# Sixteen of the 22 inner blocks of a feed-forward layer read a normed operand instead of the raw one

## The chip, the cores and the metric

One NeuronCore of a Trainium2 chip runs the whole program as one launch. The metric is the device time in microseconds (us), taken as the median of the runs. All operands are float32; products are made exact by splitting each operand into a high part and a low part with a shorter mantissa (hi, lo) and taking three matmuls, hi·hi, lo·hi and hi·lo.

## The reference, cut to what matters

The program computes two blocks in a row on 256 tokens of 1024 features. The change lies in the feed-forward part of the second block, which has two layers:

```python
for l in range(2):
    ...
    x = layer_norm(ALPHA * x + g1 * (o @ w_out[l]), ln1_g[l], ln1_b[l])
    x = layer_norm(ALPHA * x + g2 * swiglu(modulate(x, sh2, sc2), w_ffn_in[l], w_ffn_out[l]), ln2_g[l], ln2_b[l])

def modulate(x, shift, scale):
    return x * (1 + scale) + shift

def swiglu(u, w_ffn_in, w_ffn_out):
    a, b = jnp.split(u @ w_ffn_in, 2, axis=-1)
    return (jax.nn.silu(a) * b) @ w_ffn_out
```

`w_ffn_in` has 2 x 2816 columns, that is 22 blocks of 128 columns for `a` and 22 for `b`.

## The kernel before, in words

The tokens are kept transposed: the tile `xT` (in code `x`, `ax` or `z`) is [128 features, 8 feature blocks, 256 tokens]. At the end of the output projection a layer norm stands between `xT` and the feed-forward layer. The kernel does not wait for it. `late` (L1201) makes an operand `lh`, `ll` (hi and lo) of the tokens before their norm, with 258 columns: 256 tokens and two columns A and B of the modulation. The products of the inner layer are taken from this operand while the norm's sums, scale and offset are still being worked out. `lfin` (L1214) then finishes a product: with the norm's scale and offset (tile `ro`, one row for all partitions) it makes `t = ps * scale + offset * c` from the PSUM bank `ps` and the product's own two extra columns `c` (tiles `lt` and `lc`).

`ffn` (L1758) runs over 22 inner blocks j. For each it loads 1 MB of weights (tile `w`), splits them in two halves in `wload` (L271: `wh` by ScalarE, `wl` by VectorE; four buffers each), takes 48 matmuls into two PSUM banks (8 feature blocks x 2 x 3), and calls `fin(j)`, which has two `lfin` on VectorE, a Silu on ScalarE into tile `hj` (two buffers), a last VectorE instruction that multiplies into `hj`, and `evac` (L256), which splits the result: `hidh` on ScalarE and `hidl` on GpSimd (POOL). After most blocks one step of `modcol` (tiles `wd`, `macc`: a VectorE instruction over 1024 columns that prepares a later modulation) is put behind the last VectorE instruction of `fin`. `fin(j)` also takes one step of `apply` (L1314): for one feature block of `xT` two POOL instructions multiply by the scale and add the offset, and a third one multiplies by `ag` and adds `ab`. These 24 POOL instructions bring `xT` itself through the norm, eight steps in eight blocks.

Four loops over the 22 hidden blocks (the outer layer, from `hidh`, `hidl`) and the next norm follow.

The order on every engine is set when the program is built, by a scheduler in the recording layer that sees all the engines' queues; it may put an instruction ahead of others that the code wrote earlier. On the chip each engine goes through its own list in that order. The helpers have one line each: L236 is every matmul, L309 every ScalarE activation, L319, L322, L314 and L316 are the VectorE and POOL instructions with two inputs, three inputs, and one input with one or two scalars, and L396 the weight loads.

Of the kernel before, what the change touches and what calls it, by code (L numbers as in the profile page):

```python
# [21 lines left out]
# rows of 128 that become per-partition columns on the chip  # L22
# [15 lines left out]
# column order of the second block's input projection: 10 chunks of 256 columns  # L38
def _r(*p):
    return sum([list(range(a, b)) for a, b in p], [])  # L40
# [3 lines left out]
    _r((1152, 1408)),                                                       # linear attention: q | k  # L44
    _r((1408, 1664)),                                                       # its v
    _r((1952, 2016), (2144, 2208), (2336, 2464)),                           # grouped q, heads 0 3 | k
    _r((2016, 2080), (2208, 2272), (2080, 2144), (2272, 2336)),             # grouped q, heads 1 4 | 2 5
    _r((384, 640)),                                                         # neighbourhood k
    _r((0, 256)),                                                           # q
    _r((640, 768), (256, 384)),                                             # k | q  # L50
    _r((768, 1024)),                                                        # v
    _r((1024, 1152), (2464, 2592)),                                         # v | grouped v
    _r((1664, 1920)),                                                       # gate of the linear attention
]
# rows of the second block's output projection: query heads j and 3 + j share a tile
_WOR = list(range(640)) + sum(
    [list(range(640 + 64 * j, 704 + 64 * j)) + list(range(832 + 64 * j, 896 + 64 * j)) for j in range(3)], [])
# column order of the first block's input projection: 14 chunks of 256 columns
# [3 lines left out]
# rows of the gates on the chip: forget | input, forward heads at 0, backward heads at 32  # L62
# [3 lines left out]
def _consts():  # L66
# [4 lines left out]
    # persistent constants  # L71
# [28 lines left out]
    # masks of the levels of the linear attention  # L100
# [7 lines left out]
    # constants of the first block  # L108
# [6 lines left out]
    # frequencies at the middles of a grid of 512; tokens about their middle, folded  # L115
# [11 lines left out]
    z = np.concatenate([tl[:, None], np.cos(bw), -np.sin(bw)], -1).astype(f)   # 256, 33  # L127
# [8 lines left out]
def _layout(i):  # L136
    """numpy only moves data here"""
# [56 lines left out]
    # relative position bias as [token, key], one constant outside the window  # L194
# [8 lines left out]
    o["bias"] = pad[:, :, idx].reshape(2, 6, 2, 128, 256).transpose(0, 3, 1, 2, 4)   # l p h tt s  # L203
# [4 lines left out]
class _W:  # L208
    """a weight tile in parts of four slices"""
# [9 lines left out]
class _B:  # L219
    """one launch: both blocks"""  # L220
# [17 lines left out]
    def mx(self, out, L, R, sl, sr, start=True, stop=True):  # L238
        """one product of operands that are whole (x,) or split exactly (hi, lo)"""
        if len(L) == 1:  # L240
            self.mm(out, sl(L[0]), sr(R[0]), start, stop)
            return
        (lh, ll), (rh, rl) = [sl(x) for x in L], [sr(x) for x in R]
        self.mm(out, lh, rh, start, False)
        self.mm(out, ll, rh, False, False)
        self.mm(out, lh, rl, False, stop)

    def split(self, pool, x, tag, bufs, eng=None):
        """x = hi + lo, each with float32r's mantissa"""
# [6 lines left out]
    def evac(self, st, dst, i, x, eng=None):  # L256
        """x into slice i of an operand"""
# [6 lines left out]
    def op8(self, st, tag):  # L264
        """an operand tile [128, 8, 256]"""
# [20 lines left out]
    def bank(self, ps, w, u, q, order=range(8), half=None):  # L286
        """two blocks of 128 columns into one bank, over half of the eight row tiles: q is 0 or 4"""
# [9 lines left out]
    def pin(self, after):  # L297
        """issue what follows after these instructions, each on its own engine"""
# [41 lines left out]
    # per-token statistics of a transposed tile: sums over the feature axis as columns  # L340
# [5 lines left out]
    def rows(self, ps, colv):  # L346
        """columns [tok, 2] -> the same row on every partition [128, 256]"""
# [10 lines left out]
    def toT(self, psp, dst, src):  # L358
        """[tok, 2, 1024] -> [128, 8, 256]"""
# [13 lines left out]
    def fromT(self, psp, dst, src):  # L373
        """[128, 8, 256] -> [tok, 2, 1024]"""
# [24 lines left out]
    def modvec(self, psp, wd, lhs, bias, outs, groups, get=None):  # L399
        """lhs [128, 8, 32] against wd (1024, 6144), 1024 columns a group; outs: list of (column tile, replica)"""  # L400
# [9 lines left out]
    def modout(self, pool, psp, ps, bias, outs, g):  # L410
        """a group's products, 256 columns on each quarter of the partitions, as columns"""
# [14 lines left out]
    def modcol(self, pool, psp, wd, v, bias, out, groups):  # L426
        """column tile v [128, 8] against wd (1024, 6144), 1024 columns a group: products summed over the row tiles on
        the vector engine, then over the partitions on the tensor engine"""
# [17 lines left out]
    def run(self):  # L446
        nc, tc, d = self.nc, self.tc, self.d
        self.wbufs = {"w": 4, "wm": 4, "wx": 2, "wb": 3, "wd": 2, "split": 4}
        with ExitStack() as es:
# [5 lines left out]
            with tc.tile_pool(name="ps", bufs=1, space=PSUM) as self.pp, \  # L455
# [11 lines left out]
                with tc.tile_pool(name="M", bufs=1) as mp, tc.tile_pool(name="WB", bufs=1) as self.wb:  # L467
                    self.moe_route(mp, pm)
                    with tc.tile_pool(name="X", bufs=1, side="right") as xp:
                        # the context's part of the second block runs between the experts' loads  # L470
# [57 lines left out]
    def phase_a(self, ap, pm, pa):  # L528
        nc, d, cp = self.nc, self.d, self.cp
        T, P = self.T, self.P  # L530
# [13 lines left out]
        # the first two groups of the modulation: buffers that nothing else needs yet  # L544
# [20 lines left out]
        o = 0  # L565
# [66 lines left out]
        def half(w, b):  # L632
            """half of the rows of a weight tile, split"""
# [1329 lines left out]
```

## Time and profile before

| | us |
|---|---|
| median of 3 runs | 2240.02 (2239.44 to 2242.13) |
| span of the profiled execution | 2234.8 |
| so around the span, against the median | 5.2 |
| first feed-forward layer, first matmul to last | about 1644.6 to 1850 |
| second feed-forward layer, first matmul to last | about 2020.8 to 2226 |
| TensorE busy in the span | 1976.9 (88%) |
| VectorE busy | 967.5 (43%) |
| ScalarE busy | 630.5 (28%) |
| POOL busy | 294.9 (13%) |

The profile is of one execution; its own time outside the profiler is not listed apart from the three runs, so the span and the 5.2 us around it stand for it. Times in the rows are microseconds from the start of the span. "PEclk" is the granted share of TensorE's full clock. The two feed-forward layers lie 376.2 us apart and run through the same sequence.

### The profile page before, as it was taken

The page shows a single profiled execution, that of the slowest core. Times are in us where ns is not written, and L with a number is a line of the kernel's source. Part 1 is how long each engine was busy: PE and PEld are TensorE (multiplying, and loading weights), DVE is VectorE, ACT ScalarE, POOL GpSimd, SP SyncE. Part 2 cuts the span into 40 slices and gives each one's busy share as a digit, 9 for nine tenths or more (in the row PEclk, how much of TensorE's full clock was granted, in tenths as well). Part 3 has the DMA queues.
Part 4 walks back from the last instruction along what each step waited for, and adds up shares of the span by engine and source line. Part 5 has one row for each costly group of instructions (what it writes and reads, how often), then busy time and mean ns, then how long its engine had stood idle before and what let it go on. Part 6 is the DMA issues. An engine that isn't in the chain of part 4 may idle for free.

```text
span 2234.8 us, 33003 instructions
## 1 busy us (share of the span) xinstructions
PE 1976.9 (88%) x13588; PEld 1373.1 (61%) x13588; DVE 967.5 (43%) x1919; ACT 630.5 (28%) x1091; POOL 294.9 (13%) x334
## 2 busy tenths in 40 slices
PE   7999879987888989988898977679999998998998
PEld 2777744542345545545455531167789998778998
DVE  3665422124402101110012111159679888868974
ACT  3434321012401000000001100055545446554543
POOL 0012000001000000000000000044044216206311
PEclk9999979998988999999999987689999999999999
DMA  9677789998897999999998999963246674214652
GB/s 347 245 294 285 260 315 411 414 417 303 332 411 306 414 414 416 417 414 414 414 417 339 404 414 418 417 223 111 92 148 226 230 240 156 99 67 170 227 198 86
DMA packets 133479, 666.31 MB, mean 298 GB/s; under 512 B 14608, under 2 KB 18128, under 8 KB 86800
## 3 DMA queue, kind: packets, MB, share of 16 engines
q1 hardware_dynamic: 132192, 660.38, 76.1%
q0 software_dynamic: 1136, 3.82, 0.5%
q8 instruction: 107, 1.75, 0.3%
q14 instruction: 44, 0.36, 0.0%
HBM read 663.10 MB, written 1.05 MB: 297 GB/s over the span
## 4 chain that ended last, share of the span: by engine, by line
PE 54%; DMA 27%; DVE 9%; ACT 3%; POOL 3%; issue 3%; SPq 0%; POOLq 0%; ACTq 0%; DVEq 0%
PE ps L236 52%; DMA wm<-in_w_f 8%; DMA w<-in_w_up 5%; DMA wb<-in_w_up 4%; PE ps L306 2%; DMA w<-in_w_down 2%; DMA wb<-in_w_down 2%; POOL xT L319 2%; DVE wl L319 1%; DMA wm<-in_w_in 1%; DMA wb<-in_w_gate 1%; DMA w<-in_w_gate 1%; DVE ll L322 1%; DMA wm<-in_w_ada 1%; DMA wd<-in_w_ada 1%
## 5 line engine op out<-in xcount | busy, mean ns | idle before, releaser
L236 PE MATMUL ps<-u,wm 128*128 128x256 f32 (+1 forms) x1168 | 279.5, 400 | 8.9 <-DMA wm<-in_w_f 5.4
L236 PEld LDWEIGHTS ps<-u,wm 128*128 128x128 f32 (+1 forms) x1168 | 228.0, 198 | 78.3 <-DMA wm<-in_w_f 17.3
L319 DVE TENSOR_TENSOR wl<-w,wh 128x1024 fp32r<-128x1024 f32 (+1 forms) x194 | 239.8, 1244 | 54.8 <-ACT wh L309 54.4
L236 PE MATMUL ps<-lh,wh 128*128 128x258 f32 x848 | 244.7, 289 | 7.6 <-DVE lt L319 7.6
L236 PE MATMUL ps<-ll,wh 128*128 128x258 f32 x848 | 244.3, 288 | 5.1 <-DVE ll L322 5.1
L236 PE MATMUL ps<-lh,wl 128*128 128x258 f32 x848 | 243.8, 288 | 5.6 <-DVE wl L319 4.1
L309 ACT ACTIVATE wh<-w 128x1024 fp32r<-128x1024 f32 (+1 forms) x196 | 200.1, 1029 | 164.4 <-PE ps L236 155.1
L236 PE MATMUL ps<-w,xsel 128*32 128x512 f32 x1176 | 182.7, 666 | 38.2 <-DMA w<-in_w_up 25.1
L319 DVE TENSOR_TENSOR hid<-hid,ps 128x256 f32<-128x256 f32 (+1 forms) x38 | 20.2, 533 | 392.4 <-ACT hid L309 241.2
L236 PEld LDWEIGHTS ps<-lh,wh 128*128 128x128 f32 x848 | 164.1, 194 | 9.9 <-ACT wh L309 8.0
L236 PEld LDWEIGHTS ps<-lh,wl 128*128 128x128 f32 x848 | 164.4, 194 | 6.7 <-DVE wl L319 5.2
L236 PEld LDWEIGHTS ps<-ll,wh 128*128 128x128 f32 x848 | 164.7, 194 | 6.2 <-DVE ll L322 6.1
L236 PE MATMUL ps<-wb,xsel 128*32 128x512 f32 x872 | 136.8, 657 | 35.1 <-DMA wb<-in_w_up 22.1
L309 ACT ACTIVATE hid<-ps 128x256 f32<-128x256 f32 (+1 forms) x38 | 18.0, 473 | 402.1 <-PE ps L236 395.8
L236 PEld LDWEIGHTS ps<-w,xsel 128*32 128x32 f32 x1176 | 31.9, 113 | 136.3 <-DMA w<-in_w_up 62.2
L1112 POOL COPY px<-Pg 128x256 f32<-128x256 f32 x16 | 6.4, 397 | 803.7 <-PE ps L306 783.7
L322 DVE SCALAR_TENSOR_TENSOR xT<-ps,mod,xT 128x256 f32<-128x256 f32 x168 | 72.9, 478 | 77.6 <-PE ps L236 77.6
L236 PE MATMUL ps<-w,hidT 128*32 128x512 f32 x584 | 82.0, 650 | 26.7 <-DMA w<-in_w_down 21.7
L236 PE MATMUL ps<-hidh,wl 128*128 128x256 f32 x352 | 98.6, 280 | 1.6 <-DVE wl L319 1.6
L236 PE MATMUL ps<-hidh,wh 128*128 128x256 f32 x352 | 98.8, 281 | 0.0
L236 PE MATMUL ps<-hidl,wh 128*128 128x256 f32 x352 | 98.2, 279 | 0.0
L236 PEld LDWEIGHTS ps<-wb,xsel 128*32 128x32 f32 x872 | 23.5, 112 | 103.5 <-DMA wb<-in_w_up 50.3
(474 smaller groups left out, 3696.1 us busy)
## 6 DMA issues: line engine op xcount, KB each, us to landing
w<-in_w_gate SPq DMA_DIRECT2D x74, 1024.0 KB, 16.0
w<-in_w_up SPq DMA_DIRECT2D x73, 1024.0 KB, 15.4
w<-in_w_down SPq DMA_DIRECT2D x73, 1024.0 KB, 16.2
w<-in_w_f SPq DMA_DIRECT2D x60, 1024.0 KB, 4.9
wb<-in_w_up SPq DMA_DIRECT2D x55, 1024.0 KB, 15.4
wb<-in_w_down SPq DMA_DIRECT2D x55, 1024.0 KB, 15.8
wb<-in_w_gate SPq DMA_DIRECT2D x54, 1024.0 KB, 15.5
wm<-in_w_ada SPq DMA_DIRECT2D x76, 512.0 KB, 6.3
```

The costliest lines, as they stand in the source:

```text
L236: self.lm = self.nc.tensor.matmul(out, lhsT, rhs, start=start, stop=stop)
L306: self.nc.tensor.transpose(out, in_, self.ident[:k, :k])
L309: self.nc.scalar.activation(out, in_, func, **kw)
L319: return (eng or self.nc.vector).tensor_tensor(out, a, b, op)
L322: return (eng or self.nc.vector).scalar_tensor_tensor(out, in0, s, in1, op0, op1)
L1112: nc.gpsimd.tensor_copy(px.rearrange("p t (r s) -> p t r s", r=4), self.Pg[:, :, e, :].unsqueeze(2).to_broadcast([128, 2, 4, 32]))
```

## The change

`ffn` makes a second operand `un` (tiles `AT` for hi and `ul` for lo, 256 columns). `apply` is now called with it: beside its three POOL instructions, each of its eight steps has a ScalarE instruction that writes the hi part of a block of `un` from the normed `xT`, a VectorE instruction (tile `Pm`) that forms the same value in full, and a second one that subtracts to give the lo part `ul`. Each `fin` takes two steps of `apply` instead of one, and what is left is taken before block 6. Blocks 0 to 5 still use the raw operand, blocks 6 to 21 use `un`, with 256 columns, and need no `lfin`: Silu is read from one PSUM bank and one VectorE instruction multiplies by the other.

```diff
     def norm(self, p, psp, z, sqtag, put=None):
...
-        sq = self.T(p, [128, 8, 256], sqtag)
+        sq = None
...
         def feed(k=None):
+            nonlocal sq
             g = nc.gpsimd
+            if sq is None:
+                sq = self.T(p, [128, 8, 256], sqtag)
...
     def ffn(self, st, l, u, ax, g, feed=None):
         p, psp, d = st["p"], st["g"], self.d
+        nl = 6
+        if st["r3"]:
+            un = (self.T(st["ap"], [128, 8, 256], st["atag"], 1, F32R), self.T(p, [128, 8, 256], "ul", 1, F32R))
...
         def fin(j, pp):
             h = self.T(p, [128, 256], "hj", 2)
-            t, c = self.lfin(p, pp[0], ro)
-            self.act(h, t, AF.Silu, bias=c)
-            t, c = self.lfin(p, pp[1], ro)
-            e = self.stt(h, t, c, h, ALU.add, ALU.mult)
+            if j < nl:
+                t, c = self.lfin(p, pp[0], ro)
+                self.act(h, t, AF.Silu, bias=c)
+                t, c = self.lfin(p, pp[1], ro)
+                e = self.stt(h, t, c, h, ALU.add, ALU.mult)
+            else:
+                self.act(h, pp[0][:, 0:256], AF.Silu)
+                e = self.tt(h, h, pp[1][:, 0:256], ALU.mult)
             self.evac(st, hid, j, h, self.nc.gpsimd)
...
-            next(app, None)
+            for _ in range(2):
+                next(app, None)
         for j in range(22):
...
                 pp = [self.P(psp), self.P(st["S"])]
+                if j == nl:
+                    self.all(app)
+                v, n = (u, 258) if j < nl else (un, 256)
...
-                            self.mx(pp[b][:, 0:258], w, u, lambda x: x[:, k, 128 * b:128 * b + 128], lambda x: x[:, k],
+                            self.mx(pp[b][:, 0:n], w, v, lambda x: x[:, k, 128 * b:128 * b + 128], lambda x: x[:, k],
                                     k == 0, k == 7)
...
-                            app = self.apply(p, ax, ro, st["cf"])
+                            app = self.apply(p, ax, ro, st["cf"], un)
...
+            self.pk = "DDDDDDDD"
             with self.tc.tile_pool(name=f"CF{l}", bufs=1, reuse_waits="tile") as fp:
...
-                sm = dict(st, p=fp, extra=extra, cf=cf, ro=ro)
+                sm = dict(st, p=fp, po=fp, extra=extra, cf=cf, ro=ro)
```

Beside this the tile `Pm` of `apply` has 256 columns instead of 512, and comments are gone. The change moves instructions on every engine at the start of the feed-forward layer. Three places are shown, all of the first layer; the second has the same order.

On POOL, from the end of the norm on. `xT<-xT,ro` is the norm of a block of the tokens (two instructions a block), `xT<-xT,cfg,cfb` the third instruction of an `apply` step, `hidl` the low part of a finished hidden block. Before:

```order
L319 TENSOR_TENSOR xT_11_85<-xT_11_85,ro_1999_10345 128x256 x4
L316 TENSOR_SCALAR xT_11_85<-xT_11_85,cfg1616_1617_8387,cfb1617_1618_8388 128x256 x2
L319 TENSOR_TENSOR xT_11_85<-xT_11_85,ro_1999_10345 128x256 x4
L316 TENSOR_SCALAR xT_11_85<-xT_11_85,cfg1616_1617_8387,cfb1617_1618_8388 128x256 x2
L319 TENSOR_TENSOR xT_11_85<-xT_11_85,ro_1999_10345 128x256 x4
L316 TENSOR_SCALAR xT_11_85<-xT_11_85,cfg1616_1617_8387,cfb1617_1618_8388 128x256 x2
L319 TENSOR_TENSOR xT_11_85<-xT_11_85,ro_1999_10345 128x256 x3
L319 TENSOR_TENSOR hidl_1979_10243<-hj_2000_10347,hidh_1978_10242 128x256
```

And with the change:

```order
L319 TENSOR_TENSOR xT_11_85<-xT_11_85,ro_2000_10346 128x256 x10
L316 TENSOR_SCALAR xT_11_85<-xT_11_85,cfg1616_1617_8387,cfb1617_1618_8388 128x256
L319 TENSOR_TENSOR xT_11_85<-xT_11_85,ro_2000_10346 128x256 x6
L316 TENSOR_SCALAR xT_11_85<-xT_11_85,cfg1616_1617_8387,cfb1617_1618_8388 128x256 x2
L319 TENSOR_TENSOR hidl_1980_10244<-hj_2001_10348,hidh_1979_10243 128x256
```

The first `hidl` stood behind 15 instructions of two inputs and 6 of one; it now stands behind 16 and 3.

On VectorE, around the last instruction of `fin` of block 2 (`hj_2019` before, `hj_2024` with the change). `wl_2027`, `wl_2029` before and `wl_2034`, `wl_2036` with the change are the two halves of the low weights of block 3; `wl_2039`, `wl_2041` and `wl_2048`, `wl_2050` are those of block 4. Before, all four stand ahead of `hj_2019`, whose last rows are:

```order
L319 TENSOR_TENSOR wl_2029_10511<-w_2025_10504,wh_2028_10510 128x1024
L322 SCALAR_TENSOR_TENSOR hj_2005_10401<-lt_2009_10410,lc_2008_10408,hj_2005_10401 128x256
L314 TENSOR_SCALAR macc_2010_10416<-wd_2011_10417,lhs2_36_140 128x1024
L1218 COPY lc_2020_10484<-ps2017_10433 128x2
L319 TENSOR_TENSOR lt_2021_10486<-ps2017_10433,ro_1999_10345 128x256
L319 TENSOR_TENSOR wl_2039_10585<-w_2037_10582,wh_2038_10584 128x1024
L322 SCALAR_TENSOR_TENSOR lt_2021_10486<-ro_1999_10345,lc_2020_10484,lt_2021_10486 128x256
L1218 COPY lc_2022_10490<-ps2018_10434 128x2
L319 TENSOR_TENSOR lt_2023_10492<-ps2018_10434,ro_1999_10345 128x256
L319 TENSOR_TENSOR wl_2041_10589<-w_2037_10582,wh_2040_10588 128x1024
L322 SCALAR_TENSOR_TENSOR lt_2023_10492<-ro_1999_10345,lc_2022_10490,lt_2023_10492 128x256
L322 SCALAR_TENSOR_TENSOR hj_2019_10483<-lt_2023_10492,lc_2022_10490,hj_2019_10483 128x256
```

With the change:

```order
L316 TENSOR_SCALAR Pm_2031_10533<-xT_11_85,cfA1614_1615_8385,cfB1615_1616_8386 128x256
L322 SCALAR_TENSOR_TENSOR hj_2024_10506<-lt_2028_10515,lc_2027_10513,hj_2024_10506 128x256
L322 SCALAR_TENSOR_TENSOR macc_2013_10428<-wd_2029_10521,lhs2_36_140,macc_2013_10428 128x1024
L319 TENSOR_TENSOR ul_1978_10242<-Pm_2031_10533,AT_1977_10241 128x256
L319 TENSOR_TENSOR wl_2034_10541<-w_2032_10538,wh_2033_10540 128x1024
L319 TENSOR_TENSOR wl_2036_10545<-w_2032_10538,wh_2035_10544 128x1024
L316 TENSOR_SCALAR Pm_2044_10615<-xT_11_85,cfA1614_1615_8385,cfB1615_1616_8386 128x256
L316 TENSOR_SCALAR Pm_2045_10622<-xT_11_85,cfA1614_1615_8385,cfB1615_1616_8386 128x256
L319 TENSOR_TENSOR ul_1978_10242<-Pm_2044_10615,AT_1977_10241 128x256
L319 TENSOR_TENSOR ul_1978_10242<-Pm_2045_10622,AT_1977_10241 128x256
L319 TENSOR_TENSOR wl_2048_10630<-w_2046_10627,wh_2047_10629 128x1024
L319 TENSOR_TENSOR wl_2050_10634<-w_2046_10627,wh_2049_10633 128x1024
```

The four low halves of blocks 3 and 4 have gone from ahead of the last instruction of `fin(2)` to behind it; ahead of it stand six `Pm` and five `ul` of the new operand.

On TensorE, at the start of block 3 (`ps2037` and `ps2038` are its PSUM banks, `ps2051` and `ps2052` those of block 4), with the change:

```order
L236 MATMUL ps2023_10457<-ll_1941_9920,wh_2020_10452 128x258
L236 MATMUL ps2037_10548<-lh_1940_9919,wh_2033_10540 128x258
L236 MATMUL ps2038_10549<-lh_1940_9919,wh_2033_10540 128x258
L236 MATMUL ps2051_10637<-lh_1940_9919,wh_2047_10629 128x258
L236 MATMUL ps2052_10638<-lh_1940_9919,wh_2047_10629 128x258
L236 MATMUL ps2037_10548<-lh_1940_9919,wl_2034_10541 128x258
```

The second matmul of block 3 needs `wl_2034`, and all later ones of the program stand behind it; four first matmuls (two of block 3, two of block 4) stand ahead of it. Before, the matmuls of block 3 stood one behind the other.

## Rows read from the trace of the kernel before

**Rows 1.** The page, part 1: busy time of the engines in the span.

```profile
PE 1976.9 (88%) x13588; PEld 1373.1 (61%) x13588; DVE 967.5 (43%) x1919; ACT 630.5 (28%) x1091; POOL 294.9 (13%) x334
```

**Rows 2.** Busy time in stretches: PE, PEld, DVE, ACT, POOL (instructions), PEclk, DMA share, GB/s.

```profile
1764.00:1778.00 14.00, 14.00 (x119) 14.00 (x118) 12.69 (x23) 7.02 (x10) 3.35 (x3) 1.00 0.62 200
1658.58:1678.26 19.68, 19.68 (x166) 19.64 (x164) 15.24 (x23) 6.92 (x9) 19.68 (x22) 1.00 0.43 159
```

**Rows 3.** Timeline of TensorE at its stall, first layer, then second layer.

```profile
1678.16 0.28 PE L236 MATMUL ps<-ll,wh 128*128 128x258 f32 x1
1682.24 0.55 PE L236 MATMUL ps<-lh,wh 128*128 128x258 f32 x1 [3.81 <-DVE lt L319]
1683.79 0.58 PE L236 MATMUL ps<-lh,wl 128*128 128x258 f32 x1 [0.99 <-DVE wl L319]
...
2054.35 0.28 PE L236 MATMUL ps<-ll,wh 128*128 128x258 f32 x1
2058.42 0.36 PE L236 MATMUL ps<-lh,wh 128*128 128x258 f32 x1 [3.79 <-DVE lt L319]
2059.96 0.58 PE L236 MATMUL ps<-lh,wl 128*128 128x258 f32 x1 [1.19 <-DVE wl L319]
```

**Rows 4.** Who waited for whom, 1658 to 1690: total us, times, longest.

```profile
ACT hj L309 <- POOL hidl L319: 9.8, 1, 9.8
DVE hj L322 <- ACT hj L309: 5.7, 1, 5.7
PEld ps L236 <- ACT wh L309: 4.0, 1, 4.0
```

**Rows 5.** Timeline of POOL, end of the norm to the first hidden block.

```profile
1658.58 4.25 POOL L319 TENSOR_TENSOR xT<-xT,ro 128x256 f32<-128x256 f32 x4 [2.52 <-ACT ro L309]
...
1676.17 2.12 POOL L319 TENSOR_TENSOR xT<-xT,ro 128x256 f32<-128x256 f32 x3
1678.26 0.72 POOL L319 TENSOR_TENSOR hidl<-hj,hidh 128x256 fp32r<-128x256 f32 x1
```

**Rows 6.** Groups of POOL instructions, 1658.5 to 1678.3: count, busy us, mean ns.

```profile
L319 POOL TENSOR_TENSOR xT<-xT,ro 128x256 f32<-128x256 f32 x15 | 14.7, 1010 | 2.5 <-ACT ro L309 2.5
L316 POOL TENSOR_SCALAR xT<-xT,cfg,cfb 128x256 f32<-128x256 f32 x6 | 5.1, 858 | 0.0
```

**Rows 7.** Timeline of POOL, start of the second layer's mixers.

```profile
1860.10 8.49 POOL L319 TENSOR_TENSOR xT<-xT,ro 128x256 f32<-128x256 f32 x9 [3.49 <-ACT ro L309]
```

**Rows 8.** Timeline of DVE: first layer's stall, then mixers of the second layer.

```profile
1679.55 0.94 DVE L322 SCALAR_TENSOR_TENSOR hj<-lt,lc,hj 128x256 f32<-128x256 f32 x1 [5.73 <-ACT hj L309]
1680.41 1.28 DVE L322 SCALAR_TENSOR_TENSOR macc<-wd,lhs,macc 128x1024 f32<-128x1024 f32 x1
...
1684.92 1.21 DVE L319 TENSOR_TENSOR wl<-w,wh 128x1024 fp32r<-128x1024 f32 x1
...
1885.62 0.73 DVE L316 TENSOR_SCALAR Pm<-xT,cfA,cfB 128x256 f32<-128x256 f32 x2
```

**Rows 9.** TensorE, timeline: 68 matmuls of 258 columns, then 70 of 256, first and last.

```profile
1759.83 0.28 PE L236 MATMUL ps<-lh,wl 128*128 128x258 f32 x1
...
1767.89 0.28 PE L236 MATMUL ps<-ll,wh 128*128 128x258 f32 x1
...
1807.76 0.28 PE L236 MATMUL ps<-hidh,wl 128*128 128x256 f32 x1
...
1815.89 0.28 PE L236 MATMUL ps<-hidh,wl 128*128 128x256 f32 x1
```

**Rows 10.** Granted clock after the stall, first and second layer: PE, PEclk, DMA share, GB/s.

```profile
1680.90:1687.80 6.90, 4.57 (x20) 0.51 0.35 93
...
2059.80:2063.20 3.40, 3.23 (x15) 0.50 0.29 113
```

**Rows 11.** VectorE groups, 1450 to 2235: count, busy us, mean ns of one.

```profile
L322 DVE SCALAR_TENSOR_TENSOR lt<-ro,lc,lt 128x256 f32<-128x256 f32 x88 | 46.3, 530 | 2.1
L319 DVE TENSOR_TENSOR lt<-ps,ro 128x256 f32<-128x256 f32 x88 | 36.2, 415 | 4.6 <-ACT ro L309 4.6
```

More of the change, by code (lines that the diff above doesn't have):

```diff
@@ L1321, in apply @@
             if u and self.pk[k] == "A":
-                y = self.T(p, [128, 512], "Pm", 3)[:, 0:256]
+                y = self.T(p, [128, 256], "Pm", 3)
                 self.stt(y, z[:, k], A[:, k:k + 1], r, ALU.mult, ALU.mult)
@@ L1333, in apply @@
             if u and self.pk[k] != "A":
-                y = self.T(p, [128, 2, 256], "hsq", 1)[:, 0] if self.pk[k] == "P" else self.T(p, [128, 512], "Pm", 3)[:, 0:256]
+                y = self.T(p, [128, 2, 256], "hsq", 1)[:, 0] if self.pk[k] == "P" else self.T(p, [128, 256], "Pm", 3)
                 self.act(u[0][:, k], z[:, k], AF.Identity, scale=A[:, k:k + 1], bias=B[:, k:k + 1])
```

## The prediction

> **What bounds the kernel now.** I read the page's first part, then busy time by stretches, then TensorE's timeline where the second view shows it not full, then the waits and the other engines' timelines around that place. TensorE is busy for 88% of the span [rows 1]. Inside the feed-forward layers it is full nearly throughout: in a stretch of steady blocks it is busy 14.00 of 14.00 us while VectorE is busy 12.69 and POOL 3.35 [rows 2]. There, only fewer or shorter matmuls can save time.
>
> The exception is the start of each layer. TensorE starts a matmul at 1678.16, the next at 1682.24 and the one after it, which needs a low weight half, at 1683.79 [rows 3]; the second layer repeats this 376.2 us later. These are the first matmuls of block 5, since blocks 3 and 4 ran before the hole. The cause is a chain of single waits [rows 4]: ScalarE waited 9.8 us for POOL to take `hidl` of block 0 out of `hj` (two buffers, so block 2 needs that of block 0), VectorE then waited 5.7 us for ScalarE's `hj`, and TensorE waited 4.0 us for weights that stood behind `hj` on ScalarE. POOL itself was full from 1658.58 to 1678.26, 19.68 of 19.68 us [rows 2], with 15 two-input instructions in 14.7 us and 6 one-input ones in 5.1 us [rows 6]. So POOL's queue ahead of the first `hidl` sets the hole; what VectorE and TensorE have queued behind block 2's `fin` sets its price.
>
> **The change, part by part.**
>
> Columns: in 16 blocks of each layer a matmul has 256 columns instead of 258. That is 16 x 48 = 768 matmuls a layer. From first to last, 67 steps of 258 columns take 8.06 us, 120.3 ns each, and 69 steps of 256 columns 8.13 us, 117.8 ns each [rows 9]. The gain is 768 x 2.5 ns = 1.9 us a layer, all of it on the path, since TensorE is full there. The Trainium skill ("TensorE: Matmul & The Clock Gate", "Back-to-back issue gap") gives an isolated matmul N / 2.4 ns and a constant. Two columns would be an estimated 0.8 ns by it, or 0.6 us a layer; the trace's spacing differs, and it decides.
>
> VectorE's relief: the same blocks lose two `lfin` each. Per block that is two instructions of 0.415 us and two of 0.530 us [rows 11], about 30 us a layer. I cost it at nothing: TensorE is already full beside that work [rows 2]. What is late next there is TensorE itself.
>
> The new operand: 8 ScalarE and 16 VectorE instructions a layer. A `Pm` costs 0.37 us in the rows for the mixers [rows 8]; the subtraction is of the kind at 0.415 us [rows 11]. By themselves they are 6 us of VectorE. What matters is where they stand: they need normed blocks, which POOL delivers one at a time, and the order has put six `Pm` and five `ul` ahead of the last instruction of `fin(2)`, and both low halves of blocks 3 and 4 behind it. TensorE's list holds four first matmuls that need high halves alone, and then one that needs block 3's `wl`. So TensorE now stops after block 2 and four matmuls, and must wait for a chain that in the old order had 96 matmuls beside it.
>
> When that chain ends: the norm is on chip at 1658.58, where POOL starts [rows 5]. Now 16 two-input and 3 one-input instructions stand ahead of `hidl`. At the rates of the old stretch, 14.7 / 15 = 0.98 and 5.1 / 6 = 0.85 us [rows 6], they take 15.7 + 2.6 = 18.3 us, to 1676.9. Nine two-input instructions in 8.49 us in the mixers [rows 7] say 0.94, the same within 0.6 us in all. `hidl` takes 0.72 [rows 5]: 1677.6. In the old run, from the end of `hidl` (1678.26 + 0.72 = 1678.98) over `hj` on ScalarE and VectorE to the end of `macc` (1680.41 + 1.28 = 1681.69) took 2.7 us [rows 5, 8]; the same instructions follow now. Then one `ul` (0.4) and the low half (1.21 [rows 8]) add 1.6. The low half is there at 1677.6 + 2.7 + 1.6 = **1681.9**.
>
> Against the old run, which took its own second matmul of block 5 at 1683.79, TensorE restarts 1.9 us earlier but two blocks behind. It has 96 matmuls more to do, less the three that now run early, 93 x 0.1203 = 11.2 us. Nothing else can run in the hole, since TensorE's list is in order. After the old hole the granted clock is 0.51 for 6.9 us in the first layer and 0.50 for 3.4 us in the second, the lower of its two levels (1.2 of 2.4 GHz) [rows 10], after 4 us without matmuls. The new hole is some 15 us long; I take the same loss after it, so no difference, and as a bound one more slow stretch of 3.4 us, which costs half of itself, 1.7 us. POOL's and ScalarE's other moves, the DMAs of weights (now queued behind two `macc` loads on SP) and the rest of the order have slack behind the restart: the four buffers of split weights let the engines run two blocks, 11 us, ahead. The last block of `un` is ready a few us after the restart, and block 6 comes 136 matmuls later.
>
> Sum a layer: -1.9 + 11.2 - 1.9 = +7.4 us; two layers +14.8. The sum is a difference in the profiled execution, whose span is 2234.8; the median, 5.2 us above it, I move by the same amount: 2240.0 + 14.8 = **2254.8**.
>
> Bounds of the unknown, POOL's pace beside VectorE. Undisturbed, three two-input instructions took 2.12 us, 0.71 each [rows 5]. All 19 at that pace take 13.5 us; the low half is ready at 1677.1, and a layer loses 2.6 us. The other end adds up the work of both engines: beside the 13.5 us, VectorE has 6 `Pm` (2.2), 5 `ul` (2.1), 6 `lt` and 2 `hj` at 0.53 (4.2) and a `macc` (1.28), 9.8 us in all. That puts the low half at 1686.9 and the loss at 12.4. I take the pace of the old stretch because VectorE was busy 15.24 of 19.68 us there [rows 2], and its instructions now in the same stretch add up to about as much.
>
> **The rivals.**
>
> *POOL and VectorE exclude each other.* If no VectorE instruction with two inputs in SBUF can run beside a POOL instruction, the upper end above holds: 2 x 12.4 = +24.8, 2264.8. For it: POOL's pace is 0.71 beside an idle VectorE and 4.25 / 4 = 1.06 beside a busy one [rows 5]. Against it: the old stretch held 19.8 us of POOL's work and 15.24 us of VectorE's in 19.68 us [rows 2, 6]; 21 instructions at 0.71 leave under 5 us for VectorE if nothing overlapped. The Trainium skill ("SBUF — State Buffer", "Who interferes with whom") states just such a lock for the whole instruction. The trace agrees that there is contention, not that it is full. Chance 0.14.
>
> *POOL runs undisturbed.* VectorE now waits for POOL's blocks, so it could leave POOL alone more than before. Lower end: 2 x 2.6 = +5.2, 2245.2. For it: VectorE's `Pm` wait for blocks one after another. Against it: the work it has in between. Chance 0.12; about half of it would show as no change.
>
> *Faster: TensorE's restart costs nothing.* If the low half were ready before the hole costs more than the old one, only the columns count: 2 x 1.9 = -3.8, and 2236.2. The point from which it decides is 1683.8 - 11.2 = 1672.6 for the low half in the first layer. That needs POOL's first `hidl` done by 1668.3, 19 instructions and `hidl` in 9.7 us, 0.49 us each; the least the rows show is 0.71. Only a VectorE that took `wl_2034` without standing behind `hj_2024` could do it, and the order excludes that. Chance 0.05.
>
> **How the numbers follow.** The forecast case, low half between 1680 and 1684 (2251 to 2259 with both layers), has 0.69, the others as given. About 0.2%, 4.5 us, is what a measurement of this kernel can tell from no change: the three runs spread over 2.7 us. The forecast and the exclusion case are slower, and so is half of the undisturbed one: 0.69 + 0.14 + 0.06 = 0.89. The same: 0.06. Faster: the last rival, 0.05, though its gain is near the limit. The range goes from the undisturbed case less the spread of the runs, 2243, to the exclusion case with a slow stretch more in each layer, 2268.
>
> **What would show it.** In the changed kernel's profile TensorE should have a hole in each layer that begins near 1667 (96 matmuls of 0.12 us before 1678.2) and ends near 1682 (and 376 + 7 us later), broken only by four single matmuls; the matmul after it should wait for VectorE's `wl`; ScalarE's wait for `hidl` should remain, several us long; POOL should be full from 1658.6 to about 1677. The matmuls from `AT`/`ul` should stand 117 to 118 ns apart. VectorE should be well under 12 of 14 us busy in the later blocks with nothing gained by it. I am wrong if the hole ends before 1677 or after 1687, if a second hole follows at blocks 5 to 7 (weights or `un` late), or if the later blocks' spacing falls by clearly more than 2.5 ns.

## The result, and the profile after

The changed kernel takes 2251.22 us (median, 2246.95 to 2256.14); the kernel before, beside it, 2239.44 us. The ratio of the runs is 1.0063, with a 95% interval of 1.0049 to 1.0078, so +14.1 us; the quotient of the two medians is 1.0053, or +11.8 us, and lies in that interval. The forecast was 2254.8 us, +14.8, and slower. The span of the profiled execution is 2244.8 us, 10.0 more than before.

The page's first part, after. VectorE has lost 31.5 us of busy time against [rows 1]; the span grew all the same:

```profile
PE 1972.9 (88%) x13588; PEld 1366.1 (61%) x13588; DVE 936.0 (42%) x1759; ACT 637.4 (28%) x1107; POOL 285.4 (13%) x334
```

Busy time in two stretches (PE, PEld, DVE, ACT, POOL with their instructions, PEclk, DMA share, GB/s), after. The first answers to the second row of [rows 2], from the start of POOL's work to the end of the first `hidl`; the second is a stretch of steady blocks:

```profile
1657.03:1673.33 16.30, 9.56 (x74) 8.82 (x72) 15.10 (x28) 10.27 (x16) 16.30 (x21) 0.84 0.09 29
1764.00:1778.00 14.00, 14.00 (x122) 14.00 (x121) 9.24 (x10) 7.06 (x11) 2.31 (x2) 1.00 0.78 269
```

In the steady blocks VectorE fell from 12.69 to 9.24 us and TensorE is as full as before. At the layer's start TensorE is busy for 9.56 of 16.30 us, where it was full before, and VectorE for 15.10.

TensorE's timeline at the hole, first layer, after (as [rows 3]):

```profile
1665.05 0.28 PE L236 MATMUL ps<-ll,wh 128*128 128x258 f32 x1
1665.96 0.69 PE L236 MATMUL ps<-lh,wh 128*128 128x258 f32 x2 [0.63 <-DVE lt L319]
1672.75 1.09 PE L236 MATMUL ps<-lh,wh 128*128 128x258 f32 x2 [6.11 <-DVE lt L322]
1678.20 0.58 PE L236 MATMUL ps<-lh,wl 128*128 128x258 f32 x1 [4.36 <-DVE wl L319]
1678.58 0.42 PE L236 MATMUL ps<-ll,wh 128*128 128x258 f32 x1
```

The hole lies two blocks earlier than the old one, from 1665 to 1678.2, and lets four first matmuls through. It ends with the low half `wl` of block 3. After it matmuls start 0.22 us apart until 1681.7, at a granted clock of 0.50, the lower of the two levels, and then 0.12 apart.

Who waited for whom, 1655 to 1700, after (as [rows 4]; total us, times, longest):

```profile
PEld ps L236 <- ACT wh L309: 6.3, 1, 6.3
PE ps L236 <- DVE lt L322: 6.1, 1, 6.1
PE ps L236 <- DVE wl L319: 4.4, 1, 4.4
DVE Pm L316 <- POOL xT L319: 1.2, 2, 0.6
ACT hj L309 <- POOL hidl L319: 0.7, 1, 0.7
```

ScalarE's 9.8 us behind `hidl` have shrunk to 0.7. The wait that ends the hole is for VectorE's `wl`; in the 6.1 us before it TensorE's weight load also waited for ScalarE's `wh`. VectorE hardly waits.

Timelines of POOL and then of VectorE, after (as [rows 5] and [rows 8]):

```profile
1657.03 7.82 POOL L319 TENSOR_TENSOR xT<-xT,ro 128x256 f32<-128x256 f32 x10 [3.52 <-ACT ro L309]
1664.86 0.96 POOL L316 TENSOR_SCALAR xT<-xT,cfg,cfb 128x256 f32<-128x256 f32 x1
1665.80 5.32 POOL L319 TENSOR_TENSOR xT<-xT,ro 128x256 f32<-128x256 f32 x6
1671.11 1.36 POOL L316 TENSOR_SCALAR xT<-xT,cfg,cfb 128x256 f32<-128x256 f32 x2
1672.44 0.89 POOL L319 TENSOR_TENSOR hidl<-hj,hidh 128x256 fp32r<-128x256 f32 x1
```

```profile
1656.98 0.76 DVE L319 TENSOR_TENSOR lt<-ps,ro 128x256 f32<-128x256 f32 x2 [3.28 <-ACT ro L309]
...
1661.12 0.95 DVE L319 TENSOR_TENSOR ul<-Pm,AT 128x256 fp32r<-128x256 f32 x1
...
1665.06 0.41 DVE L319 TENSOR_TENSOR ul<-Pm,AT 128x256 fp32r<-128x256 f32 x1
...
1674.34 0.94 DVE L322 SCALAR_TENSOR_TENSOR hj<-lt,lc,hj 128x256 f32<-128x256 f32 x1
1675.20 1.28 DVE L322 SCALAR_TENSOR_TENSOR macc<-wd,lhs,macc 128x1024 f32<-128x1024 f32 x1
1676.40 0.61 DVE L319 TENSOR_TENSOR ul<-Pm,AT 128x256 fp32r<-128x256 f32 x1
1676.93 2.35 DVE L319 TENSOR_TENSOR wl<-w,wh 128x1024 fp32r<-128x1024 f32 x2
```

POOL needs 15.4 us for its 19 instructions. An `ul` takes 0.95 us once and 0.41 another time, though nothing about it differs but what POOL is doing: a two-input instruction at 1661.12, a one-input one at 1665.06.

**One number for every kernel.** From the first matmul after the norm's rows to the first matmul of the outer layer TensorE does the same inner blocks in all kernels here. I call it the inner time. TensorE's timeline shows both ends; first layer, before, then after, then the kernel b_pin of the experiments:

```profile
1657.62 0.36 PE L236 MATMUL ps<-lh,wh 128*128 128x258 f32 x1
...
1784.61 0.28 PE L236 MATMUL ps<-hidh,wh 128*128 128x256 f32 x1
```

```profile
1656.07 0.37 PE L236 MATMUL ps<-lh,wh 128*128 128x258 f32 x1
...
1788.34 0.28 PE L236 MATMUL ps<-hidh,wh 128*128 128x256 f32 x1
```

```profile
1654.27 0.36 PE L236 MATMUL ps<-lh,wh 128*128 128x258 f32 x1
...
1774.02 0.28 PE L236 MATMUL ps<-hidh,wh 128*128 128x256 f32 x1
```

| kernel | inner time, layer 1 / layer 2, us | ratio to the kernel before (95%) |
|---|---|---|
| before | 126.99 / 126.66 | 1 |
| change | 132.27 / 132.41 | 1.0063 (1.0049 to 1.0078) |
| b_pin | 119.75 / 119.75 | 0.9933 (0.9915 to 0.9951) |
| b_hj4 | 122.63 / 122.62 | 0.9967 (0.9951 to 0.9983) |
| a_split | 126.48 / 126.24 | 1.0008 (0.9992 to 1.0023) |
| a_short | 128.15 / 128.00 | 1.0017 (0.9998 to 1.0035) |
| b_dve | 128.26 / 128.24 | 1.0009 (0.9993 to 1.0025) |
| a_slow | 128.87 / 129.22 | 1.0010 (0.9997 to 1.0024) |
| a_mac | 129.80 / 129.81 | 1.0052 (1.0036 to 1.0068) |
| a_pin | 130.91 / 130.54 | 1.0054 (1.0032 to 1.0077) |
| a_pin2 | 131.33 / 130.65 | 1.0052 (1.0035 to 1.0068) |
| a_hj4 | 132.38 / 132.77 | 1.0074 (1.0057 to 1.0092) |
| a_build | 134.15 / 134.22 | 1.0076 (1.0060 to 1.0092) |

The change adds 5.28 and 5.75 us of inner time, 11.0 in all, near the lower end of the interval in us (11.0 to 17.5). Of the medians' 11.8 that leaves 0.8; the rest of the 14.1 I can't place. In the profile of after TensorE also ran at the lower clock for 6.8 and 3.4 us at the norm ahead of the layers; the profile of before has none there, but b_pin's has (3.4 and 6.8 us), so they are no mark of the change.

### The profile page after: what moved, and what is told of

Read it like the earlier page. It is cut to its first block, busy times and chain, and to the rows that moved or that the text cites. A ratio compares the mean times of both kernels' runs of the same rounds, so it can differ in the third digit from the quotient of the medians.

```text
span 2244.8 us, 32816 instructions
## 1 busy us (share of the span) xinstructions
PE 1972.9 (88%) x13588; PEld 1366.1 (61%) x13588; DVE 936.0 (42%) x1759; ACT 637.4 (28%) x1107; POOL 285.4 (13%) x334
## 4 chain that ended last, share of the span: by engine, by line
PE 56%; DMA 27%; DVE 9%; ACT 3%; issue 3%; POOL 2%; SPq 1%; POOLq 0%; ACTq 0%; DVEq 0%
PE ps L236 54%; DMA wm<-in_w_f 8%; DMA w<-in_w_up 5%; DMA wb<-in_w_up 3%; DMA wb<-in_w_down 3%; PE ps L306 2%; DMA wm<-in_w_in 2%; DMA w<-in_w_down 2%; DVE wl L319 1%; DMA w<-in_w_gate 1%; POOL xT L319 1%; DMA wb<-in_w_gate 1%; DVE ll L322 1%; DMA wm<-in_w_ada 1%; DMA wd<-in_w_ada 1%
## 5 line engine op out<-in xcount | busy, mean ns | idle before, releaser
L236 PE MATMUL ps<-u,wm 128*128 128x256 f32 (+1 forms) x1168 | 271.3, 392 | 8.7 <-DMA wm<-in_w_f 6.1
L236 PEld LDWEIGHTS ps<-u,wm 128*128 128x128 f32 (+1 forms) x1168 | 222.4, 193 | 76.2 <-DMA wm<-in_w_f 16.7
L236 PE MATMUL ps<-ul,wh 128*128 128x256 f32 x736 | 207.4, 282 | 0.0
L236 PE MATMUL ps<-AT,wl 128*128 128x256 f32 x512 | 144.8, 283 | 0.0
L236 PE MATMUL ps<-AT,wh 128*128 128x256 f32 x512 | 143.4, 280 | 0.0
L236 PEld LDWEIGHTS ps<-ul,wh 128*128 128x128 f32 x736 | 138.3, 188 | 4.3 <-issue 4.3
L236 PE MATMUL ps<-lh,wh 128*128 128x258 f32 x336 | 101.1, 303 | 13.5 <-DVE lt L322 12.2
L236 PE MATMUL ps<-lh,wl 128*128 128x258 f32 x336 | 100.0, 299 | 13.7 <-DVE wl L319 12.2
L236 PE MATMUL ps<-ll,wh 128*128 128x258 f32 x336 | 100.6, 301 | 5.2 <-DVE ll L322 5.1
## 6 DMA issues: line engine op xcount, KB each, us to landing
w<-in_w_up SPq DMA_DIRECT2D x73, 1024.0 KB, 15.4
w<-in_w_down SPq DMA_DIRECT2D x73, 1024.0 KB, 16.3
```

The source lines that it names most:

```text
L236: self.lm = self.nc.tensor.matmul(out, lhsT, rhs, start=start, stop=stop)
```

## The experiments

My theory after the traces was the prediction's: the order at the layer's start makes the hole. POOL's queue ahead of `hidl`, and `Pm` that waits for POOL, stand in front of the low halves. The rivals: the operand's own work on VectorE costs, or the use of the operand does. Names that begin with a_ start from the changed kernel, b_ from the kernel before.

**a_pin2 and b_pin: POOL's order alone.**

```diff
-            self.evac(st, hid, j, h, self.nc.gpsimd)
+            v = self.evac(st, hid, j, h, self.nc.gpsimd)
...
-            for _ in range(2):
-                next(app, None)
+            with self.tc.issue_after(v.ins):
+                for _ in range(2):
+                    next(app, None)
```

(b_pin: the same with one `next`, in the kernel before.)

> The changed kernel with POOL's order alone altered: each block's hidl goes ahead of the normalisation that is issued after it, so VectorE's Pm and ul come later too and the low weight halves of block 3 stand ahead of them. Operand, its two steps a block, six late blocks and all columns as in the change. Theory (the loss is the order at the layer's start): both the new hole of about 13 us and the older one of about 5.5 us a layer go, with the half-clock stretch behind them; against the kernel before -2 x (5.5 + 2.5) for its own hole and -3.8 for the columns, about 2220, and anything under 2232 supports it. No idle time of TensorE over 1 us in the first four blocks after the norm. Rival (the operand's own work on VectorE and ScalarE, or a late operand at block 6, is what costs): 2245 or more, with a wait for ul or wl that stays.

> The kernel before with the same reordering of POOL (hidl ahead of the normalisation of that block), no new operand, 258 columns throughout. Theory: the old hole goes, about -16 us, 2223; it stands some 4 us above the changed kernel with the same reordering, the columns' part. Rival (the old hole has another cause than POOL's queue, as the low halves' place): 2236 or more.

b_pin did what was expected: 0.9933, -15 us, and in the inner blocks TensorE never stops. a_pin2 did not: 1.0052, 2247 instead of some 2220 us. The wait only changed its name. Timeline of VectorE in a_pin2, at the first `Pm` of each of three blocks:

```profile
1666.63 0.81 DVE L316 TENSOR_SCALAR Pm<-xT,cfA,cfB 128x256 f32<-128x256 f32 x1 [1.32 <-POOL xT L319]
...
1672.90 0.80 DVE L316 TENSOR_SCALAR Pm<-xT,cfA,cfB 128x256 f32<-128x256 f32 x1 [2.01 <-POOL xT L319]
...
1681.07 0.80 DVE L316 TENSOR_SCALAR Pm<-xT,cfA,cfB 128x256 f32<-128x256 f32 x1 [2.37 <-POOL xT L319]
```

With `hidl` first, POOL normalises later, and `Pm` stands in VectorE's list before its block is there. So far the theory of waits could still hold, with `Pm` in the place of `hj`. But TensorE's loss in this kernel is 11.6 us of inner time against b_pin, and these waits are 5.7 us, 7.0 with a fourth.

**a_hj4 and b_hj4: more buffers.**

```diff
-            h = self.T(p, [128, 256], "hj", 2)
+            h = self.T(p, [128, 256], "hj", 4)
```

> The changed kernel with four hj buffers instead of two, so that ScalarE's hj of block 2 need not wait for POOL's hidl of block 0. The rows after show ScalarE waiting 0.66 us there and VectorE busy 15.1 of 16.3 us. Theory now (VectorE's own list, stretched by the work on POOL, sets when the low half is ready): within 2 us of the changed kernel, 2249 to 2253, and the hole ends within 1 us of where it did. Rival (the path of the prediction's sum: POOL's 19 instructions, hidl, hj): block 2 goes on without POOL, the low half comes several us earlier, 2236 to 2246.

> The kernel before with four hj buffers instead of two, POOL's order untouched. Theory (in the kernel before the hole is ScalarE's hj waiting for POOL's hidl through two buffers): hole gone as in b_pin, -14 us, ratio about 0.9935. Rival (POOL's load beside VectorE makes the hole, the buffers don't, as in a_hj4): ratio over 0.998.

In the kernel before the buffers were most of the hole: 4.4 and 4.0 us less inner time, ratio 0.9967, where I had expected the 7 us of b_pin. In the changed kernel they did nothing, 132.38 and 132.77 us. Timeline of ScalarE, a_hj4: `hj` of block 2 starts without a wait, and nothing comes of it, since the low half's `wl` started 20.0 us after VectorE's first `lt` (1672.84 against 1652.88) as in the change (1676.93 against 1656.98).

```profile
1668.67 0.51 ACT L309 ACTIVATE hj<-lt,lc 128x256 f32<-128x256 f32 x1
```

So the chain that the prediction summed, POOL, `hidl`, `hj`, does not set the end of the new hole. The chain of work that ended last in the change's own trace, followed back from TensorE's restart, says the same (start us, us, what):

```profile
1657.03 5.65 POOL xT L319 x7
1662.68 0.03 issue
1662.71 0.04 DVE Pm L316
...
1676.48 0.54 DVE ul L319
1677.01 1.15 DVE wl L319
```

POOL is in it for the first seven normalising instructions only, until a `Pm` has its block; from 1662.71 on it is VectorE's list alone, with no `hidl` in it, and the second layer has the same. The two chains lay close together. ScalarE's timeline, after, has block 2's `hj` done at 1673.87, and VectorE came to its own `hj` at 1674.34, 0.5 us later:

```profile
1673.36 0.51 ACT L309 ACTIVATE hj<-lt,lc 128x256 f32<-128x256 f32 x1 [0.66 <-POOL hidl L319]
```

**a_build: the operand made, but not used.**

```diff
-            if j < nl:
+            if True:
...
-                v, n = (u, 258) if j < nl else (un, 256)
+                v, n = u, 258
```

> The changed kernel that builds the normed operand but does not use it: all 22 blocks take the operand not yet normed, with 258 columns and lfin, as in the kernel before. Theory: the same hole as in the change and none of the columns' gain, 2251 + 3.8 = 2255; matmuls of blocks 6 to 21 at 120.3 ns again instead of 117.5. Rival (VectorE's relief in the later blocks is worth something): over 2260. Rival (the loss lies in using the operand, not in building it): near 2240.

The inner time is 1.88 and 1.81 us longer than in the change, the columns' price to a tenth. VectorE is back at 12.62 of 14 us in the steady blocks, and that costs no more than the columns. The loss lies in building the operand. (The ratio, 1.0076, has an interval too wide to show 3.7 us by itself.)

**a_short: less of POOL, the same VectorE.**

```diff
-            self.tt(z[:, k], z[:, k], r, ALU.mult, g)
+            self.tt(z[:, k, 0:n], z[:, k, 0:n], r[:, 0:n], ALU.mult, g)
...
-                            app = self.apply(p, ax, ro, st["cf"], un)
+                            app = self.apply(p, ax, ro, st["cf"], un, 64)
```

(The add of the offset likewise. 192 of the 256 columns of each block are left without the norm.)

> The changed kernel in which POOL's multiply by the norm's scale and add of its offset take 64 of 256 columns of each block; the rest of the residual stays unscaled, so that is left out of the computation. VectorE's list is the same instruction for instruction, hidl stands as before. Theory (VectorE's list ahead of the low half is some 15 us of work at the undisturbed lengths, 0.41 us for a subtraction, and 21 us in the change because POOL's work stretches it): the hole ends 4 to 6 us earlier a layer, -8 to -12 us against the change, ratio to the kernel before 1.001 to 1.003; VectorE's subtractions of 128x256 in that stretch take 0.41 instead of up to 0.95 us. Rival (VectorE's list is as long by itself, whatever POOL does): the change's 1.0063.

VectorE's list is the same, instruction for instruction. Its timeline, a_short: the first `lt`, two instructions for which the change needed 0.95 and 0.94 us, and the low halves.

```profile
1664.14 0.76 DVE L319 TENSOR_TENSOR lt<-ps,ro 128x256 f32<-128x256 f32 x2 [3.91 <-ACT ro L309]
...
1666.39 0.54 DVE L319 TENSOR_TENSOR ul<-Pm,AT 128x256 fp32r<-128x256 f32 x1
...
1676.28 0.47 DVE L322 SCALAR_TENSOR_TENSOR hj<-lt,lc,hj 128x256 f32<-128x256 f32 x1
...
1678.40 2.87 DVE L319 TENSOR_TENSOR wl<-w,wh 128x1024 fp32r<-128x1024 f32 x2
```

From the first `lt` to `wl` it is 14.3 us here and 20.0 in the change: 5.7 us of the hole are VectorE's instructions stretched by POOL, and its waits for POOL. The ratio, 1.0017, lies where it was expected. This does not tell stretching from waiting, but VectorE's waits were 1.2 us. POOL's queue ahead of `hidl` is shorter here too; that this queue does not set the end of the hole is what a_hj4 shows.

**a_mac: less of VectorE, the same POOL.**

```diff
-                if j % 3:
+                if j % 3 and j > 5:
                     next(extra, None)
```

> The changed kernel without the modulation's column sums (macc) in blocks 1 to 5; they come from block 7 on. Ahead of block 3's low half VectorE's list loses two macc of 1.21 and 1.28 us, and the low half moves ahead of block 2's hj and one ul (0.94 and 0.61 us). Theory (VectorE's list ahead of the low half sets the hole's end): the hole ends 2.5 to 4 us earlier a layer, -5 to -8 us against the change, ratio to the kernel before 1.0025 to 1.004. Rival (POOL's blocks or hidl set it): unchanged, 1.0063.

TensorE's timeline at the hole, a_mac:

```profile
1672.74 0.80 PE L236 MATMUL ps<-lh,wh 128*128 128x258 f32 x2 [8.03 <-ACT wh L309]
1673.33 0.52 PE L236 MATMUL ps<-lh,wl 128*128 128x258 f32 x1
```

The first matmul with a low half starts 2.9 us earlier, 19.2 us after the first matmul (1673.33 against 1654.14; change 1678.20 against 1656.07, 22.1), and the inner time falls by 2.5 and 2.6 us. The ratio, 1.0052, is a little above the expected range, and its interval reaches the change's. VectorE's list does bear on the end, POOL's queue ahead of the first `hidl` being as it was. It no longer bears on it alone: TensorE's wait ends with ScalarE's `wh`, which stands behind a `hj` that waited 1.7 us for `hidl`. With 2.9 us less on VectorE the other chain holds as well.

**a_pin and a_split: less in one block, or later.** a_pin is a_pin2 with one step of `apply` a block and ten raw blocks:

```diff
-        nl = 6
+        nl = 10
...
-                for _ in range(2):
-                    next(app, None)
+                next(app, None)
```

a_split takes `apply` apart and has seven raw blocks:

```diff
+            with self.pin((v,)):
+                for _ in range(2):
+                    next(app, None)
+            if j >= 2:
+                with self.pin((e, s, v)):
+                    for _ in range(2):
+                        next(bld, None)
```

Here `app` normalises on POOL, `bld` builds the operand and does POOL's last step, and e, s, v are block j's last instruction on VectorE, ScalarE and POOL.

> As a_pin2 but with one step of normalising and building a block instead of two, and ten blocks with the operand not yet normed. In a_pin2 VectorE waited 1.3, 2.0 and 2.4 us at Pm for four two-input instructions of POOL each, and TensorE stopped for 3.7 and 3.1 us behind it. Theory (each Pm issued with its own block's normalisation waits for two POOL instructions instead of four, half as long, and VectorE has less work a block): the stops shrink to 0 to 3 us a layer, -6 to -14 us against the kernel before, ratio 0.994 to 0.997. Rival (any such Pm in front of wl costs a hole as large): ratio 1.003 or more.

> The changed kernel with the normalisation and the building of the operand taken apart: after each hidl POOL normalises two blocks; Pm, ul, the AT rows and POOL's last step on a block come two blocks of the inner layer later, behind that block's hj on VectorE; seven blocks instead of six take the operand not yet normed. Theory (what costs is VectorE's list standing behind Pm that waits for POOL's block; the operand itself is cheap): no hole, as in b_pin (0.9933 of the kernel before, -15 us), and the columns of 15 blocks on top, 2 x 15 x 48 x 2.5 ns = 3.6 us: -18 us, ratio about 0.992. Rival (building the operand costs TensorE something wherever it stands): no better than b_pin, ratio 0.9933 or more, with waits for wl that return in blocks 3 to 7.

Both expectations fell, and what their rivals named came instead. a_pin cut the stop into seven of 0.4 to 2.5 us, and the loss stayed nearly whole, 11.2 and 10.8 us over b_pin. In a_split no `Pm` waits any more, and it still costs 6.7 and 6.5 us of inner time over b_pin, though its columns save 1.8. Who waited, a_split, 1653 to 1735:

```profile
PE ps L236 <- DVE wl L319: 3.8, 3, 1.7
PE ps L236 <- DVE ul L319: 1.0, 1, 1.0
```

**b_dve: VectorE's work alone.** What was left was VectorE's time itself. Busy time in b_pin over six blocks' length (5.8 us each) from 1665.8 on, inside block 3, the columns as above:

```profile
1665.80:1677.40 11.60, 11.60 (x99) 11.60 (x98) 11.36 (x20) 5.67 (x8) 9.52 (x9) 1.00 0.69 235
1677.40:1689.00 11.60, 11.60 (x98) 11.60 (x98) 11.49 (x18) 5.66 (x8) 10.16 (x8) 1.00 0.60 209
1689.00:1700.50 11.50, 11.50 (x98) 11.50 (x97) 11.39 (x20) 5.66 (x8) 10.06 (x9) 1.00 0.61 223
```

TensorE is full, and VectorE is full too, to 0.1 or 0.2 us in two blocks.

```diff
+            if 2 <= j < 6:
+                with self.tc.issue_after(e.ins):
+                    for k in (0, 1):
+                        y, y2 = (self.T(p, [128, 256], t, 3) for t in ("Pm", "Pn"))
+                        self.ts(y, ro[0], st["cf"][0][:, k:k + 1], st["cf"][1][:, k:k + 1], ALU.mult, ALU.add)
+                        self.tt(y2, y, ro[1], ALU.subtract)
```

> b_pin (the kernel before with hidl ahead of each normalisation, 0.9933, no hole) plus VectorE work alone: in blocks 2 to 5 two multiply-adds and two subtractions of 128x256 each, 16 instructions and some 6 us a layer, which read the norm's rows, wait for nothing of POOL's and whose results nobody reads. Theory (VectorE was busy 11.4 of 11.5 us in blocks 1 to 4 of b_pin, so it is the second bound there, and the operand's work cannot be had for nothing wherever it stands): the stretch from the norm to the first column sum, 72.5 us in b_pin, grows by 5 to 8 us, ratio 0.997 to 1.0005, as in a_split. Rival (a_split lost by late operand blocks or by order, VectorE has room): ratio 0.993 to 0.995.

It cost 8.5 us of inner time in each layer, and the ratio is 1.0009 where b_pin has 0.9933, both a little above what was expected: sixteen instructions that wait for nothing of POOL's and that nobody waits for make the whole of b_pin's gain go. They are some 6 us at undisturbed lengths, but beside POOL they ran longer. Their busy time in the inner time of the first layer (PE, PEld, DVE, ACT, these instructions alone):

```profile
1651.31:1779.57 128.26, 0.00 (x0) 0.00 (x0) 9.77 (x16) 0.00 (x0) 0.99 0.61 215
```

So 9.8 us of VectorE cost 8.5 us of TensorE. Two stretches of b_dve in which they stand:

```profile
1674.50:1686.00 11.50, 10.22 (x83) 9.81 (x81) 11.50 (x23) 4.24 (x7) 9.18 (x8) 1.00 0.62 222
1686.00:1698.00 12.00, 9.96 (x68) 9.76 (x69) 11.97 (x24) 6.34 (x9) 4.55 (x6) 0.86 0.37 139
```

VectorE is full, and TensorE is not. Over these blocks VectorE is the second bound, right under the first.

a_split fits this: its 6.7 and 6.5 us over b_pin and the 1.8 us that its columns save make 8.5 and 8.3 us, so that building the operand, freed of `Pm`'s waits, costs what b_dve's work costs, ScalarE's `AT` with it. a_build, with 258 columns throughout like b_dve, is 5.9 and 6.0 us over b_dve. That much the order of the change adds; which part of it does, POOL's, ScalarE's or VectorE's, no run tells apart.

**a_slow: later, where VectorE was taken to have room.** a_split with the building later and slower:

```diff
-        nl = 7
+        nl = 14
...
-            if j >= 2:
+            if j >= 6:
                 with self.pin((e, s, v)):
-                    for _ in range(2):
+                    for _ in range(1):
                         next(bld, None)
```

> As a_split, but with the building of the operand put off to blocks 6 to 13, one block of it at a time, so that 14 blocks take the operand not yet normed and eight the normed one. Theory (VectorE has no room in blocks 1 to 4 and about 1 us a block in the steady ones, 12.69 of 14 us busy; a step is 0.75 us): no hole, no stop later, and the columns of eight blocks, 2 x 8 x 48 x 2.5 ns = 1.9 us, under b_pin: ratio 0.991 to 0.994. Rival (VectorE is late from block 1 on and any added step stops TensorE): ratio over 0.996, with waits for wl in blocks 7 to 14.

Again not what was expected: 1.0010. The inner time is 9.1 and 9.5 us over b_pin. There are four short stops of 0.7 to 1.0 us, at blocks 7, 10, 11 and 13, and about 4.4 us in block 14, the first with the new operand (1735 to 1746):

```profile
PE ps L236 <- ACT AT L1360: 2.5, 1, 2.5
PE ps L236 <- DVE ul L319: 1.4, 2, 1.1
```

The last step stands behind block 13's `hj`, and block 14 needs it at once: there I had cut it too fine. The short stops are what the rival named. The expectation had counted the room wrongly: 12.69 of 14.00 us busy [rows 2] leaves 1.31 us in 2.4 blocks of 5.8 us, 0.54 us a block, and a step needs 0.75. And the blocks in which the building now stood are not yet steady ones. Busy time in b_pin up to block 13:

```profile
1712.00:1726.70 14.70, 14.70 (x125) 14.70 (x124) 14.52 (x28) 8.13 (x12) 6.00 (x3) 1.00 0.81 282
```

No version with the new operand came under b_pin. The version that beats both kernels is b_pin: no new operand, and `hidl` ahead of each normalisation, 2219.98 us beside 2234.40 for the kernel before.

## Why the prediction was right, and where it was not

The direction and the number held: +14.8 forecast, +14.1 measured by the ratio and +11.8 by the medians. That the number came so near is in part luck: in the inner blocks, where the prediction placed all of it, the loss is 11.0 us, and the chain that it summed is not the one that held TensorE. Step by step:

- **Columns, -1.9 us a layer.** Right: a_build gives 1.88 and 1.81.
- **VectorE's relief in the later blocks, nothing.** Right: 3.4 of 14 us less work there, TensorE full in both.
- **Where the hole lies.** Right: after block 2 and four first matmuls, ended by block 3's `wl`, no second hole. The two cases at the ends were wrong: the hole ended neither at POOL's undisturbed pace nor at the sum of both engines' work.
- **The low half at 1681.9.** Too late by 2.15 us. The changed run's norm came 1.55 us earlier (1656.07 against 1657.62), so the forecast stands for 1680.35; TensorE restarted at 1678.20. POOL took 15.4 us for its 19 instructions instead of 18.3, since 0.98 us for a two-input instruction, from [rows 6], became 13.14 / 16 = 0.82. In [rows 6] VectorE had `wl` of 1024 columns beside POOL, here none; that this is the reason was not tried. Over two layers it is -4.3, and 2254.8 - 4.3 = 2250.5.
- **The chain to the low half.** This step failed, and the number hid it. The prediction let POOL's queue, `hidl` and `hj` set the end, and wrote of the operand that its 6 us of VectorE mattered by "where they stand". ScalarE's wait for `hidl`, which "should remain, several us long", was 0.7 us. With four buffers it was gone and the hole was the same. VectorE's own list, stretched by POOL, ended 0.5 us behind the chain, and it was the one that held TensorE. That the two ended so close together was luck. a_mac and a_short shorten the list and the stretching, and the low half comes 2.9 and 5.7 us earlier.
- **"6 us of VectorE" beside other work.** Here is the cause. In the kernel before, VectorE's 5.7 us behind `hj` [rows 4] looked like room. b_pin takes that wait away, and VectorE is busy 11.4 of 11.5 us. b_dve puts some 6 us of work in, which takes 9.8 beside POOL, and loses 8.5. The order of the change made the loss larger: its inner time is 4.0 and 4.2 us over b_dve's in spite of its columns. b_dve starts from b_pin; the same work in the kernel before, with its wait, was not run.
- **The clock.** As taken: 3.5 and 3.9 us at 0.50 after the restart, beside 4.0 us (1683.79 to 1687.80) and 3.2 us (2059.96 to 2063.20) after the old one [rows 3, 10].
- **Contention not full.** The prediction showed this by adding busy times, 19.8 and 15.24 us in 19.68. That is no proof, because busy time holds the stretching too: `ul` counts 0.95 us beside POOL. At undisturbed lengths (POOL 0.71 for a two-input instruction, 0.55 for a one-input one) the stretch after holds 16 x 0.71 + 3 x 0.55 + 0.72 = 13.7 us of POOL's work; VectorE's 13 `Pm`, `ul`, `hj` and `macc` and five scalings that read only SBUF come to some 8 us. That is 21.7 in 16.3 us, so some overlap stays.

## What to carry to other kernels

Before costing an added instruction at nothing, look for the wait that makes its engine look idle, and ask how full the engine is once that wait is gone: two engines can both be at their limit with only one of them showing it. When a summed chain ends near another one, test which of the two holds by taking one away; a number that fits does not tell. And where an engine's queue mixes work that is due at once with work that is not, put the first in front: that alone was worth 15 us here.

## What was not expected of the hardware

Beside POOL's two-input instructions, VectorE's short ones with all operands in SBUF took about twice as long, and those that read PSUM did not. In the change's timeline `ul` takes 0.95 us and `hj` 0.94. Where POOL was at a one-input instruction or idle it is 0.41 (`ul` at 1665.06, beside POOL's 0.96 us from 1664.86) and 0.47 (`hj` in a_short), while two `lt` from PSUM took 0.76 us in all, 0.38 each, with POOL at work. The Trainium skill ("SBUF — State Buffer", "Who interferes with whom") says that VectorE and POOL share one pair of ports under a lock, and that work with two SBUF inputs falls under it. The rows agree on which instructions suffer. `Pm`, with one tensor input, suffered too (0.75 to 0.81 us against 0.37).

So a length from a quiet stretch understates what an instruction costs beside POOL: the work of b_dve, some 6 us by such lengths, took 9.8 us and cost TensorE 8.5. Part of the 8.5 is the lower clock after a stop, 0.86 on average in the stretch from 1686 to 1698.
